# The small operations of the heads' norms on GpSimd instead of VectorE

## The chip, the cores and the metric

One core of one Trainium2 chip runs the whole program. The metric is the device time of one execution in microseconds. Lower is better.

## What is computed

Two blocks follow each other on a sequence of 1024 tokens of width 1024. The change lies in the first, an attention block with two kinds of heads: 8 heads of kind A (a window of 128 tokens each way, 2 heads of keys and values, rotary positions) and 8 heads of kind B (a neighbourhood on a grid, a bias by relative place). Both also see 256 context tokens. Ahead of the scores every head of q and k is normalised over its 64 columns:

```
q_a = _axial_rope(_rms_norm(q_a, qn_a), row_pos, col_pos)
k_a = _axial_rope(_rms_norm(k_a, kn_a), row_pos, col_pos)
q_b, k_b = _rms_norm(q_b, qn_b), _rms_norm(k_b, kn_b)
def _rms_norm(x, g):
    y = x * rsqrt(mean(x * x, axis=-1) + 1e-6)
    return y * g
```

Behind the attention come the output projection, a gated feed-forward product, and the second block.

## The kernel before, in words

Products are done in pairs of fp32r numbers, a high part and the rest, so a projection of one tile of 128 tokens is 8 slices of k with three matmuls each (`mm3`, L159 to L161).

The attention runs in six rounds (`ROUNDS`): A, B, B, B, B, A. In each, `Round.proj` projects ten tiles of 128 tokens: two of the context, eight of x. An A tile of x has 5 heads to normalise (4 of q, 1 of k), a B tile 4; a context tile has only its k, 1 or 2 heads. That makes 60 tiles, each of which calls `qk_prep` (L380). In it

- VectorE multiplies the projection by the gains (`yg`, L389 or L392), ScalarE squares it (L395), VectorE sums the squares of each head (`ssq`, L396);
- `rstd_of` (L138) makes the factor of each head: VectorE makes the mean (`ms`, L140), ScalarE takes the logarithm and the exponential (L142, L144), and VectorE does one Newton step in three operations (L146, L147, L149) on tiles of 128 by 1 to 5 columns;
- in A tiles of x GpSimd applies the rotary tables in four operations (L400, L405 twice, L407);
- VectorE multiplies by the factor (L409), ScalarE rounds the high part (L411), VectorE takes the rest (L412). Then PE transposes k and q (L491, L502).

While round r+1 is projected, the jobs of round r (one per head and tile of queries) are done: scores on PE (L548), a reduction for the maximum on VectorE (L555, L560, L563, L566), the exponential on ScalarE (L569), transposes on PE (L582), their split by ScalarE and VectorE (L592, L593), the product with v (L606), its sum (L612, L613) and a transposition back (L620). The transposes of a tile are handed in `TR_LAG` = 3 jobs after its projection. During the last round the weights of the output projection are prepared too, partly on GpSimd (L754, L172, on 128 by 1024).

`rstd_of` has two other kinds of callers, which stay as they are: the norms of whole rows (L275 and, for the first two tiles, ahead of the output projection) and the second block (L1510). Each engine does its instructions in one order. The program text gives a priority, and a scheduler with costs of its own sets the final order of each engine when the program is built, so an edit in one helper can move instructions everywhere in the stretch.

Of the kernel before, what the change touches and what calls it, by code (L numbers as in the profile page):

```python
# [12 lines left out]
ALU = mybir.AluOpType  # L13
# [8 lines left out]
HD = 64  # L22
# [5 lines left out]
EPS = 1e-6  # L28
# [52 lines left out]
def net_kernel(ctx: ExitStack, tc: tile.TileContext, I: dict, out: bass.AP):  # L81
    nc = tc.nc
    sync = nc.sync
    dve = nc.vector
    act = nc.scalar
    pool = nc.gpsimd
# [37 lines left out]
    def fview(ap):  # L124
        return ap.bitcast(F32)
# [9 lines left out]
        o, n = VECS[name]  # L135
        return vecs[:, o : o + n]

    def rstd_of(ssq, n, cols):  # L138
        ms = small.tile([P, 8], F32, tag="ms", name="ms")[:, :cols]
        dve.tensor_scalar(ms, ssq, 1.0 / n, EPS, ALU.mult, ALU.add)  # L140
        ln = small.tile([P, 8], F32, tag="ln", name="ln")[:, :cols]
        act.activation(ln, ms, AF.Ln)  # L142
        y0 = small.tile([P, 8], F32, tag="y0", name="y0")[:, :cols]
        act.activation(y0, ln, AF.Exp, scale=-0.5)  # L144
        y2 = small.tile([P, 8], F32, tag="y2", name="y2")[:, :cols]
        dve.tensor_tensor(y2, y0, y0, ALU.mult)  # L146
        dve.scalar_tensor_tensor(y2, y2, -0.5, ms, ALU.mult, ALU.mult)  # L147
        r = small.tile([P, 8], F32, tag="r", name="r")[:, :cols]
        dve.scalar_tensor_tensor(r, y2, 1.5, y0, ALU.add, ALU.mult)  # L149
        return r  # L150

    def eng(c):
        return dve if c == "d" else pool
# [32 lines left out]
    def rstd_ssq(ssq, n, cols):  # L186
        ms = small.tile([P, 8], F32, tag="ms", name="ms")[:, :cols]
        dve.tensor_scalar(ms, ssq, 1.0 / n, EPS, ALU.mult, ALU.add)
        return rstd_sqrt(ms, cols)
# [76 lines left out]
    def norm_in(src, where="xt"):  # L266
        if where == "xt":
            xt = pro.tile([P, D], F32, tag="xt", name="xt", bufs=3)
        else:
            xt = ap1.tile([P, CTX + S], F32, tag="kT", name="xk", bufs=4)[:, :D]  # L270
        sync.dma_start(xt, src)
        junk = pro.tile([P, D], F32, tag="junk", name="junk")
        ssq = small.tile([P, 8], F32, tag="ssq", name="ssq")
        act.activation(junk, xt, AF.Square, accum_out=ssq[:, 0:1])
        r = rstd_of(ssq[:, 0:1], D, 1)  # L275
        dve.tensor_scalar(xt, xt, r, None, ALU.mult)
        return xt
# [102 lines left out]
    def qk_prep(ps, g, rtile):  # L380

        n = ps.shape[1]

        def pa(name):
            return ap1.tile([P, 5, HD], F32, tag="pa", name=name, bufs=PA_BUFS)[:, :n]

        yg = pa("yg")
        if g.shape[1] == n:
            dve.tensor_tensor(yg, ps, g, ALU.mult)  # L389
        else:  # L390
            pairs = [v.rearrange("p (a b) d -> p a b d", b=2) for v in (yg, ps)]
            dve.tensor_tensor(*pairs, g.unsqueeze(2).to_broadcast([P, n // 2, 2, HD]), ALU.mult)  # L392
        sq = pa("sq")
        ssq = small.tile([P, 8], F32, tag="ssq", name="ssq")
        act.activation(sq, ps, AF.Square)  # L395
        dve.tensor_reduce(ssq[:, :n], sq, AX.X, ALU.add)  # L396
        r = rstd_of(ssq[:, :n], HD, n)
        if rtile is not None:
            t1, t2 = pa("t1"), pa("t2")
            eng(ROPE2[0]).tensor_tensor(t1, yg, tabs[0][:, 0, rtile, :].unsqueeze(1).to_broadcast([P, n, HD]), ALU.mult)  # L400
            ys = yg.rearrange("p h (e r f) -> p h e r f", e=2, r=2)
            ts_ = t2.rearrange("p h (e r f) -> p h e r f", e=2, r=2)
            sn = tabs[0][:, 1, rtile, :].rearrange("p (e r f) -> p e r f", e=2, r=2)
            for rr in range(2):
                eng(ROPE_ENG).tensor_tensor(ts_[:, :, :, rr, :], ys[:, :, :, 1 - rr, :],  # L405
                                            sn[:, :, rr, :].unsqueeze(1).to_broadcast([P, n, 2, 16]), ALU.mult)
            eng(ROPE2[2]).tensor_tensor(t1, t1, t2, ALU.add)  # L407
            yg = t1
        eng(Y_ENG).tensor_tensor(yg, yg, r.unsqueeze(2).to_broadcast([P, n, HD]), ALU.mult)  # L409
        qk = ap1.tile([P, 5, 2, HD], F32R, tag="qk", name="qk")[:, :n]  # L410
        act.copy(qk[:, :, 0, :], yg)  # L411
        eng(QLO_ENG).tensor_tensor(qk[:, :, 1, :], yg, fview(qk[:, :, 0, :]), ALU.subtract)  # L412
        return qk

    class Round:
# [44 lines left out]
        def proj(self, t, is_ctx, later):  # L460
# [3 lines left out]
            for k in range(KT):  # L464
# [9 lines left out]
                if k < KT - 1:  # L474
                    yield
            kt = t if is_ctx else 2 + t
            h0 = nq if is_ctx else 0
            n = nh - h0
            qk = qk_prep(ps[:, h0 * 64 : nh * 64].rearrange("p (h d) -> p h d", d=HD), self.g[:, h0 * self.g.shape[1] // nh :, :],
                         t if (self.kind == "A" and not is_ctx) else None)  # L480
            for j in range(nk):
# [288 lines left out]
    for s in range(-2, nj):  # L770
# [16 lines left out]
        for i, c in enumerate(ORDER):  # L787
# [18 lines left out]
            else:  # L806
                n = -(-left // ORDER[i:].count("f"))
# [358 lines left out]
    cols = {}  # L1166
# [223 lines left out]
    class Gla:  # L1390
# [64 lines left out]
        def mix(self):  # L1455
# [52 lines left out]
            ssq = small.tile([P, 8], F32, tag="ssq", name="ssq")  # L1508
            dve.tensor_reduce(ssq[:, :4], sq.rearrange("p b (h d) -> p (b h) d", h=2), AX.X, ALU.add)
            r = rstd_of(ssq[:, :4], P, 4)  # L1510
            for h in range(4):
                cs_ = slice(h * P, (h + 1) * P)
# [144 lines left out]
    cols = {}  # L1657
# [7 lines left out]
    for t in range(NT):  # L1665
# [15 lines left out]
        ssq = small.tile([P, 8], F32, tag="ssq", name="ssq")  # L1681
        act.activation(y, ps, AF.Square, accum_out=ssq[:, 0:1])
        r = rstd_ssq(ssq[:, 0:1], D, 1)
# [156 lines left out]
```

## Time and profile before

| | us |
|---|---|
| median of 3 runs | 2499.37 |
| lowest, highest | 2494.01, 2502.66 |
| the profiled execution, its own time | 2503.15 |
| its span in the profile | 2501.4 |
| PE, VectorE, ScalarE, GpSimd busy | 2395.9, 1783.5, 1217.0, 344.1 |

The span is what the trace covers, from the first instruction to the last; 1.75 us of the execution lie around it. A busy share is a mean over stages: the attention takes about the first 670 us, the first feed-forward and everything behind it the rest. In names, POOL is GpSimd, DVE VectorE, ACT ScalarE; "idle before" is the time in which the engine stood ahead of such instructions.

### The profile page before, as it was taken

The numbers are of one execution on the slowest core, as the hardware profiler recorded it, in microseconds if no ns is written. First come the engines' busy times: TensorE is split into PE (matmuls) and PEld (weight loads), VectorE is DVE, ScalarE is ACT, GpSimd is POOL, SyncE is SP. The second block draws the span as 40 slices with busy tenths as digits, with TensorE's granted clock in tenths as the row PEclk, the third lists the DMA queues.
The fourth block names the chain that finished last, engine by engine and source line by source line (L and its number), as shares of the span: only waits on it lengthen the run. The fifth ranks groups of instructions, "written<-read, shape, count | busy, mean of one in ns | idle before, by whom it ended". The sixth has DMA issues, their size and how long they took to land.

```text
span 2501.4 us, 35470 instructions
## 1 busy us (share of the span) xinstructions
PE 2395.9 (96%) x12448; PEld 2008.3 (80%) x12448; DVE 1783.5 (71%) x3636; ACT 1217.0 (49%) x2658; POOL 344.1 (14%) x340
## 2 busy tenths in 40 slices
PE   8899999999897999999999999999989999999998
PEld 4789999988775888888788888878767888788886
DVE  6977788888866877777575943437668666677676
ACT  4777677777744332233244542346335444444442
POOL 1400000023321222222000000003102221100011
PEclk9999999999999999999999999999999999999999
DMA  7111122222331343332699540022313544599973
GB/s 267 41 47 45 52 61 60 70 83 71 118 110 53 101 139 121 124 106 89 225 333 302 191 129 17 22 59 79 104 54 126 168 145 140 197 344 329 301 241 138
DMA packets 202893, 337.89 MB, mean 135 GB/s; under 512 B 22846, under 2 KB 84174, under 8 KB 201692
## 3 DMA queue, kind: packets, MB, share of 16 engines
q1 hardware_dynamic: 200700, 328.30, 39.3%
q0 software_dynamic: 2016, 7.34, 0.9%
q8 instruction: 98, 1.61, 0.3%
q14 instruction: 79, 0.65, 0.1%
HBM read 265.03 MB, written 70.53 MB: 134 GB/s over the span
## 4 chain that ended last, share of the span: by engine, by line
PE 80%; DVE 9%; ACT 5%; DMA 2%; issue 2%; SPq 0%; POOL 0%; DVEq 0%; ACTq 0%; POOLq 0%
PE m L160 14%; PE m L161 14%; PE m L159 14%; PE acc L159 4%; PE acc L161 4%; PE acc L160 4%; PE wide L159 3%; PE wide L160 3%; PE wide L161 3%; PE acc L606 2%; PE tr L582 2%; PE wide L548 2%; ACT qT L156 1%; PE tr L160 1%; PE tr L161 1%
## 5 line engine op out<-in xcount | busy, mean ns | idle before, releaser
L159 PE MATMUL m<-T,s 128*128 128x512 f32 x1064 | 416.9, 393 | 30.5 <-ACT T L890 25.0
L160 PE MATMUL m<-T,s 128*128 128x512 f32 x1064 | 417.9, 393 | 0.0
L161 PE MATMUL m<-T,s 128*128 128x512 f32 x1064 | 417.5, 393 | 0.0
L890 ACT CAST slab<-cmb 128x1024 fp32r<-128x1024 f32 x189 | 193.1, 1047 | 261.4 <-DVE cmb L1103 111.0
L891 DVE TENSOR_TENSOR slab<-cmb,slab 128x1024 fp32r<-128x1024 f32 x189 | 229.8, 1237 | 105.3 <-ACT slab L890 100.7
L890 ACT CAST s<-raw 128x512 fp32r<-128x512 f32 x228 | 136.1, 615 | 263.3 <-PE m L161 94.8
L159 PEld LDWEIGHTS m<-T,s 128*128 128x128 f32 x1064 | 201.3, 189 | 75.9 <-ACT T L890 25.8
L891 POOL TENSOR_TENSOR s<-raw,s 128x512 fp32r<-128x512 f32 x114 | 159.3, 1399 | 617.4 <-ACT s L890 604.0
L160 PE MATMUL m<-slab 128*128 128x512 f32 x594 | 234.0, 394 | 5.9 <-DVE slab L891 5.9
L160 PEld LDWEIGHTS m<-T,s 128*128 128x128 f32 x1064 | 201.4, 189 | 44.8 <-DVE T L891 1.3
L161 PEld LDWEIGHTS m<-T,s 128*128 128x128 f32 x1064 | 201.3, 189 | 42.6
L161 PE MATMUL m<-slab 128*128 128x512 f32 x594 | 233.5, 393 | 0.0
L159 PE MATMUL m<-slab 128*128 128x512 f32 x594 | 231.0, 391 | 1.3 <-ACT slab L890 1.3
L990 DVE TENSOR_TENSOR big<-m,big 128x512 f32<-128x512 f32 x228 | 154.0, 682 | 57.8 <-PE m L161 53.2
L159 PE MATMUL acc<-wi,slab 128*128 128x384 f32 (+1 forms) x480 | 168.6, 352 | 3.0 <-DVE y L147 1.3
L160 PE MATMUL acc<-wi,slab 128*128 128x384 f32 (+1 forms) x480 | 161.5, 337 | 0.5 <-DVE wi L240 0.5
L161 PE MATMUL acc<-wi,slab 128*128 128x384 f32 (+1 forms) x480 | 160.9, 337 | 0.0
L593 DVE TENSOR_TENSOR PT<-tr,PT 128x512 fp32r<-128x512 f32 x231 | 129.3, 564 | 44.0 <-ACT PT L592 41.8
L592 ACT CAST PT<-tr 128x512 fp32r<-128x512 f32 x231 | 112.2, 489 | 65.5 <-PE acc L606 33.3
L160 PEld LDWEIGHTS m<-slab 128*128 128x128 f32 x594 | 112.9, 190 | 30.9 <-DVE slab L891 7.5
L159 PEld LDWEIGHTS m<-slab 128*128 128x128 f32 x594 | 111.9, 188 | 25.1 <-ACT slab L890 1.7
L161 PEld LDWEIGHTS m<-slab 128*128 128x128 f32 x594 | 112.8, 190 | 23.3
(455 smaller groups left out, 5288.0 us busy)
## 6 DMA issues: line engine op xcount, KB each, us to landing
cmb<-scr SPq DMA_DIRECT2D x189, 256.0 KB, 4.2
wraw<-in_w_ff_dram SPq DMA_DIRECT2D x160, 256.0 KB, 5.4
scr<-big SPq DMA_DIRECT2D x135, 256.0 KB, 4.0
wraw<-in_w_down_dram SPq DMA_DIRECT2D x110, 256.0 KB, 5.1
raw<-in_w_ff_dram SPq DMA_DIRECT2D x16, 1024.0 KB, 6.5
scr<-big SPq DMA_DIRECT2D x27, 512.0 KB, 6.7
wm<-in_w_mod_dram SPq DMA_DIRECT2D x48, 256.0 KB, 2.7
raw<-in_w_gate_dram SPq DMA_DIRECT2D x11, 1024.0 KB, 5.4
```

What stands on the lines that cost most here:

```text
L156: act.copy(out_, in_) if c == "a" else eng(c).tensor_copy(out_, in_)
L159: pe.matmul(ps, lhsT=l_hi, rhs=r_hi, start=first, stop=False)
L160: pe.matmul(ps, lhsT=l_hi, rhs=r_lo, start=False, stop=False)
L161: pe.matmul(ps, lhsT=l_lo, rhs=r_hi, start=False, stop=last)
L548: pe.matmul(Sps[:, o : o + ln], lhsT=qT[:, w_, :], rhs=R.kT[self.kh][:, src : src + ln], start=(w_ == 0), stop=(w_ == 1))
L582: pe.transpose(t[:, (j - b0) * P : (j - b0 + 1) * P], self.P_t[:, j * P : (j + 1) * P], ident)
L592: act.copy(PT[:, :, 0, :], src)
L593: dve.tensor_tensor(PT[:, :, 1, :], src, fview(PT[:, :, 0, :]), ALU.subtract)
L606: pe.matmul(OT, lhsT=R.V[self.kh][:, vt, :], rhs=self.PT[j // 4][:, j % 4].rearrange("p e t -> p (e t)"), start=(j == 0), stop=(j == nk_al ...
L890: act.copy(hi, src)
L891: eng(lo_eng).tensor_tensor(lo, src, fview(hi), ALU.subtract)
L990: dve.tensor_tensor(V[:, half], ps, getattr(self, other[0])[:, other[1]], ALU.add)
```

## The change

The call in `qk_prep` hands GpSimd to `rstd_of`. GpSimd then does the mean and the Newton step. The two fused operations of VectorE become three plain ones, so five operations on GpSimd stand for four on VectorE. The other callers keep VectorE.

```
@@ -135,18 +135,24 @@
         o, n = VECS[name]
         return vecs[:, o : o + n]
 
-    def rstd_of(ssq, n, cols):
+    def rstd_of(ssq, n, cols, e=None):
+        e = e or dve
         ms = small.tile([P, 8], F32, tag="ms", name="ms")[:, :cols]
-        dve.tensor_scalar(ms, ssq, 1.0 / n, EPS, ALU.mult, ALU.add)
+        e.tensor_scalar(ms, ssq, 1.0 / n, EPS, ALU.mult, ALU.add)
         ln = small.tile([P, 8], F32, tag="ln", name="ln")[:, :cols]
         act.activation(ln, ms, AF.Ln)
         y0 = small.tile([P, 8], F32, tag="y0", name="y0")[:, :cols]
         act.activation(y0, ln, AF.Exp, scale=-0.5)
         y2 = small.tile([P, 8], F32, tag="y2", name="y2")[:, :cols]
-        dve.tensor_tensor(y2, y0, y0, ALU.mult)
-        dve.scalar_tensor_tensor(y2, y2, -0.5, ms, ALU.mult, ALU.mult)
         r = small.tile([P, 8], F32, tag="r", name="r")[:, :cols]
-        dve.scalar_tensor_tensor(r, y2, 1.5, y0, ALU.add, ALU.mult)
+        e.tensor_tensor(y2, y0, y0, ALU.mult)
+        if e is dve:
+            dve.scalar_tensor_tensor(y2, y2, -0.5, ms, ALU.mult, ALU.mult)
+            dve.scalar_tensor_tensor(r, y2, 1.5, y0, ALU.add, ALU.mult)
+        else:
+            e.tensor_tensor(y2, y2, ms, ALU.mult)
+            e.tensor_scalar(y2, y2, -0.5, 1.5, ALU.mult, ALU.add)
+            e.tensor_tensor(r, y2, y0, ALU.mult)
         return r
 
     def eng(c):
@@ -394,7 +400,7 @@
         ssq = small.tile([P, 8], F32, tag="ssq", name="ssq")
         act.activation(sq, ps, AF.Square)
         dve.tensor_reduce(ssq[:, :n], sq, AX.X, ALU.add)
-        r = rstd_of(ssq[:, :n], HD, n)
+        r = rstd_of(ssq[:, :n], HD, n, pool)
         if rtile is not None:
             t1, t2 = pa("t1"), pa("t2")
             eng(ROPE2[0]).tensor_tensor(t1, yg, tabs[0][:, 0, rtile, :].unsqueeze(1).to_broadcast([P, n, HD]), ALU.mult)
```

On the engines that makes 240 instructions fewer on VectorE and 300 more on GpSimd; the counts of PE, ScalarE and of the DMAs stay. The order on all engines changes up to about the first feed-forward product and is the same from there on.

VectorE at a B tile (the fifth tile of x of the fourth round, from just behind its `ssq`; L409 is the product with the factor, L566 the reduction of a job's scores). Before:

```order
L485 TENSOR_TENSOR V<-acc,V 128x64
L140 TENSOR_SCALAR ms<-ssq 128x4
L613 TENSOR_TENSOR ob<-ob,acc 128x128
L563 TENSOR_REDUCE mx<-wide 128x1
L146 TENSOR_TENSOR y_5393<-y_5391 128x4
L485 TENSOR_TENSOR V<-acc,V 128x64
L147 SCALAR_TENSOR_TENSOR y_5393<-y_5393,ms 128x4
L566 ISA wide,negs<-wide,tbl,mx 128x512
L566 ISA negs 128x1
L149 SCALAR_TENSOR_TENSOR r<-y_5393,y_5391 128x4
L593 TENSOR_TENSOR PT<-tr,PT 128x4x128
L409 TENSOR_TENSOR yg<-yg,r 128x256
```

Of the change, whose lines here stand 6 further down, from its `ssq` (L402) on; L415 is the product with the factor, L572 the reduction:

```order
L402 TENSOR_REDUCE ssq<-sq 128x4
L491 TENSOR_TENSOR V<-acc,V 128x64
L619 TENSOR_TENSOR ob<-ob,acc 128x128
L569 TENSOR_REDUCE mx<-wide 128x1
L491 TENSOR_TENSOR V<-acc,V 128x64
L415 TENSOR_TENSOR yg<-yg,r 128x256
L572 ISA wide,negs<-wide,tbl,mx 128x512
L572 ISA negs 128x1
L599 TENSOR_TENSOR PT<-tr,PT 128x4x128
```

The product with the factor now stands ahead of the reduction of the scores and of the split of the transposes, with four instructions between it and `ssq` where eleven stood.

GpSimd at the third tile of x of the last round. Before:

```order
L754 TENSOR_TENSOR tbl<-tbl,g1t 128x1024
L400 TENSOR_TENSOR t_8069<-yg,rope 128x320
L405 TENSOR_TENSOR t_8070<-yg,rope 128x10x16 x2
L407 TENSOR_TENSOR t_8069<-t_8069,t_8070 128x320
L754 TENSOR_TENSOR tbl<-tbl,g1t 128x1024
L172 TENSOR_TENSOR slab<-tbl,slab 128x1024 x2
```

Of the change, where L760 is what L754 was and L178 what L172 was:

```order
L406 TENSOR_TENSOR t_8124<-yg,rope 128x320
L411 TENSOR_TENSOR t_8125<-yg,rope 128x10x16 x2
L413 TENSOR_TENSOR t_8124<-t_8124,t_8125 128x320
L141 TENSOR_SCALAR ms<-ssq 128x5
L760 TENSOR_TENSOR tbl<-tbl,g1t 128x1024 x2
L148 TENSOR_TENSOR y_8118<-y_8116 128x5
L153 TENSOR_TENSOR y_8118<-y_8118,ms 128x5
L154 TENSOR_SCALAR y_8118<-y_8118 128x5
L155 TENSOR_TENSOR r<-y_8118,y_8116 128x5
L178 TENSOR_TENSOR slab<-tbl,slab 128x1024 x2
```

The rotary operations now come ahead of both weight products, the mean follows them, and the rest of the factor comes behind both.

## Rows read from the trace of the kernel before

**Rows 1.** The page: busy time of each engine, share of the span, instructions.

```profile
PE 2395.9 (96%) x12448; PEld 2008.3 (80%) x12448; DVE 1783.5 (71%) x3636; ACT 1217.0 (49%) x2658; POOL 344.1 (14%) x340
```

**Rows 2.** Windows: stretch, length, busy us of PE, PEld, DVE, ACT, POOL, clock, DMA.

```profile
40.00:100.00 60.00, 49.70 (x271) 42.74 (x271) 55.46 (x175) 42.28 (x128) 30.03 (x39) 0.89 0.30 106
150.00:500.00 350.00, 344.08 (x2411) 323.94 (x2410) 276.16 (x900) 244.92 (x786) 7.80 (x33) 1.00 0.19 52
500.00:660.00 160.00, 144.31 (x985) 129.36 (x985) 141.03 (x375) 124.94 (x352) 53.16 (x59) 0.97 0.23 72
```

**Rows 3.** Waits of PE, 100 to 680 us: total us, times, longest.

```profile
PE tr L582 <- DVE PT L593: 4.7, 7, 1.7
...
PE tr L491 <- DVE qk L412: 3.0, 1, 3.0
```

**Rows 4.** Groups by form, 0 to 1100 us: busy us, mean ns, idle before.

```profile
L140 DVE TENSOR_SCALAR ms<-ssq 128x4 f32<-128x4 f32 x32 | 5.2, 163 | 0.0
L146 DVE TENSOR_TENSOR y<-y 128x4 f32<-128x4 f32 x32 | 5.2, 161 | 3.8 <-ACT y L144 3.6
...
L149 DVE SCALAR_TENSOR_TENSOR r<-y,y 128x4 f32<-128x4 f32 x32 | 5.0, 156 | 0.1
L147 DVE SCALAR_TENSOR_TENSOR y<-y,ms 128x4 f32<-128x4 f32 x32 | 4.9, 153 | 0.0
```

**Rows 5.** Groups by form, VectorE, 500 to 660 us (the last A round).

```profile
L149 DVE SCALAR_TENSOR_TENSOR r<-y,y 128x5 f32<-128x5 f32 x8 | 5.5, 682 | 0.0
...
L140 DVE TENSOR_SCALAR ms<-ssq 128x5 f32<-128x5 f32 x8 | 4.3, 535 | 0.0
...
L147 DVE SCALAR_TENSOR_TENSOR y<-y,ms 128x5 f32<-128x5 f32 x8 | 2.2, 275 | 0.0
...
L146 DVE TENSOR_TENSOR y<-y 128x5 f32<-128x5 f32 x8 | 2.0, 253 | 0.2
```

**Rows 6.** Timeline around one B tile: start, us, engine, line, instruction.

```profile
382.36 0.41 DVE L396 TENSOR_REDUCE ssq<-sq 128x4 f32<-128x256 f32 x1
...
383.72 0.16 DVE L146 TENSOR_TENSOR y<-y 128x4 f32<-128x4 f32 x1 [0.22 <-ACT y L144]
...
384.01 0.75 DVE L566 CUSTOM_DVE_ANT_0 wide<-wide,tbl,mx 128x512 f32<-128x512 f32 x1
...
384.97 0.91 ACT L569 ACTIVATE prob<-wide,negs 128x768 f32<-128x768 f32 x1
...
385.71 0.42 DVE L409 TENSOR_TENSOR yg<-yg,r 128x256 f32<-128x256 f32 x1
...
389.38 0.82 PE L582 MATMUL tr<-ident,prob 128*128 128x128 f32 x6
```

**Rows 7.** Timeline of POOL, 500 to 700 us.

```profile
555.04 2.37 POOL L754 TENSOR_TENSOR tbl<-tbl,g1t 128x1024 f32<-128x1024 f32 x1 [13.90 <-ACT tbl L753]
557.36 0.88 POOL L400 TENSOR_TENSOR t<-yg,rope 128x320 f32<-128x320 f32 x1
...
562.49 2.35 POOL L172 TENSOR_TENSOR slab<-tbl,slab 128x1024 fp32r<-128x1024 f32 x1
566.87 2.40 POOL L172 TENSOR_TENSOR slab<-tbl,slab 128x1024 fp32r<-128x1024 f32 x1 [2.03 <-ACT slab L169]
...
641.12 0.29 POOL L589 CAST PT<-pf 128x128 fp32r<-128x128 f32 x1
641.49 0.46 POOL L590 TENSOR_TENSOR PT<-pf,PT 128x128 fp32r<-128x128 f32 x1
```

**Rows 8.** The chain that ended last, pieces in the last A round: start, us, what.

```profile
560.39 2.16 DVE r L149
562.65 2.54 DVE t L409
...
623.95 2.07 DVE r L149
...
635.88 1.50 DVE ms L140
```

More of the change, by code (lines that the diff above doesn't have):

```diff
@@ L136, in vec, with rstd_of @@
         return vecs[:, o : o + n]
-    def rstd_of(ssq, n, cols):
+    def rstd_of(ssq, n, cols, e=None):
+        e = e or dve
         ms = small.tile([P, 8], F32, tag="ms", name="ms")[:, :cols]
-        dve.tensor_scalar(ms, ssq, 1.0 / n, EPS, ALU.mult, ALU.add)
+        e.tensor_scalar(ms, ssq, 1.0 / n, EPS, ALU.mult, ALU.add)
         ln = small.tile([P, 8], F32, tag="ln", name="ln")[:, :cols]
@@ L145, in rstd_of @@
         y2 = small.tile([P, 8], F32, tag="y2", name="y2")[:, :cols]
-        dve.tensor_tensor(y2, y0, y0, ALU.mult)
-        dve.scalar_tensor_tensor(y2, y2, -0.5, ms, ALU.mult, ALU.mult)
         r = small.tile([P, 8], F32, tag="r", name="r")[:, :cols]
-        dve.scalar_tensor_tensor(r, y2, 1.5, y0, ALU.add, ALU.mult)
+        e.tensor_tensor(y2, y0, y0, ALU.mult)
+        if e is dve:
+            dve.scalar_tensor_tensor(y2, y2, -0.5, ms, ALU.mult, ALU.mult)
+            dve.scalar_tensor_tensor(r, y2, 1.5, y0, ALU.add, ALU.mult)
+        else:
+            e.tensor_tensor(y2, y2, ms, ALU.mult)
+            e.tensor_scalar(y2, y2, -0.5, 1.5, ALU.mult, ALU.add)
+            e.tensor_tensor(r, y2, y0, ALU.mult)
         return r
@@ L396, in qk_prep @@
         dve.tensor_reduce(ssq[:, :n], sq, AX.X, ALU.add)
-        r = rstd_of(ssq[:, :n], HD, n)
+        r = rstd_of(ssq[:, :n], HD, n, pool)
         if rtile is not None:
```

## The prediction

> **What bounds the kernel now.** I read the page's busy times first: PE is busy for 2395.9 of 2501.4 us, VectorE for 71% and GpSimd for 14% [rows 1]. So PE bounds the whole, and moving work from VectorE pays only where VectorE keeps PE waiting. The windows show where that can be. From 150 to 500 us, the B rounds, PE is busy for 344.1 of 350 us and VectorE for 276.2: there is 5.9 us to win at most. From 40 to 100 us VectorE is busy for 55.5 of 60 us and PE stands for 10.3; from 500 to 660 us, the last A round, VectorE is busy for 141.0 of 160 and PE stands for 15.7 [rows 2]. These two ends are where the change can act. From the first feed-forward on nothing is moved.
>
> PE's list of waits then tells what a late head costs. Of all 60 tiles only one had PE wait for the end of a norm chain (transposes of k behind L412), for 3.0 us; the split of the transposes of the probabilities (L593) cost 4.7 us in 7 waits [rows 3]. So in nearly all tiles the chain of the norm has room, and a change of its length is mostly hidden.
>
> **The change, part by part.** The sum is made against the profiled execution, 2503.15 us, whose span is 2501.4; that execution is 3.8 us (0.15%) above the median of 2499.37, so I add the same difference to both.
>
> What VectorE gives up. At a 4-head tile the four operations take 163 + 161 + 156 + 153 = 633 ns [rows 4]. At the eight 5-head tiles of the last round they take 5.5 + 4.3 + 2.2 + 2.0 = 14.0 us, 1.75 us a tile, because some of them are held up [rows 5]. In the first round the eight 5-head tiles give between 8 x 0.63 = 5.0 and 14.0 us. The time VectorE stands for the exponential ahead of L146 goes too; at the B tile shown it is 0.22 us [rows 6].
>
> What GpSimd takes on. No GpSimd operation on so few columns is in the trace. Two inputs of 128 columns take 0.46 us and of 320 columns 0.88, so 2.2 ns a column; going from 128 columns down to 4 leaves 0.19 us. One input of 128 columns takes 0.29. The dependent one behind it starts 0.08 us after its end [rows 7]. I take 0.19 us for each of the five and 0.08 for each handover; the row at 128 columns bounds it above at 0.46, and below it cannot be under zero. GpSimd gets 60 x 5 x 0.19 = 57 us of work, with room for it.
>
> A page speaks against this: the Trainium skill, GPSIMD Engine Reference, section 4.1 (Engine selection), says elementwise operations of two inputs are about twice as slow there and belong on VectorE. At 128 columns and more the rows lean that way; at 4 columns the estimate by rows is 0.19 against VectorE's 0.16. By the page each operation would take 0.32 us, an estimate that makes each chain about 0.5 us longer and the forecast some 4 us higher.
>
> The B tiles, 40 of them. At the tile shown `ssq` ends at 382.77, and L146 starts at 383.72, as ScalarE ends the factor's exponential at about 383.7 [rows 6]. Before, L409 starts at 385.71. Now the mean goes out through GpSimd (0.08 + 0.19 + 0.08 = 0.35), which still meets ScalarE's place in its order; then four operations (4 x 0.19 + 3 x 0.08 = 1.0) and two handovers of 0.08 put the factor at 384.85. L409 can start 0.9 us earlier than before. But VectorE reaches L409 earlier still: its new order leaves four instructions behind `ssq`. The old order had these four, three of the small operations and 0.22 us of idle time before L566 started at 384.01; less the idle time and between nothing and 3 x 0.16, that is 383.3 to 383.8, and I take 383.6. VectorE stands there for 1.25 us, and saved 0.63 + 0.22 = 0.85 at most: it loses 0.4 us a tile, 16 us in 350 of which it is busy for 276, so it stays under 85%. What is queued behind L409 is late: the reduction of a job's scores (L566), which began at 384.01, now waits for L409 to end (384.85 + 0.42 = 385.27), 1.26 us later, and the exponential on ScalarE with it. PE takes the transposes of that exponential at 389.38, and it ended at 385.88 [rows 6]: 3.5 us of room against 1.3. I take **+1.5 us** for the tiles with less room, between -3 (half of the 5.9 us) and +8 (0.2 us a tile).
>
> The first 150 us. VectorE is freed of 5.0 us or more. Against it stands a wait at L409 in each of 8 A tiles, where the rotary operations and the splits of x are ahead of the factor in GpSimd's queue. As in the B tiles the wait is a little the larger, and PE, which stands for other things too, sees a part: **+1 us**, between -5 (half of PE's 10.3) and +5 (0.6 us a tile).
>
> The last A round. Here the chain that ended last runs through the moved operations themselves: L149 for 2.16 and 2.07 us, L140 for 1.50, each several times its 0.16, beside GpSimd work on 1024 columns; L409 for 2.54 beside L172 [rows 7, 8]. If all three go from the chain, that is -5.7. But one does not: behind the factor at 623.95 GpSimd's next work is again L172, which then holds L409 instead of L149; so -3.7. What comes: at the tile of 554 us two products of 2.37 us (L754) now stand between mean and Newton step. L400 started as L754 ended, so the rotary part can move up by 2.37 at most, from an end near 560.2 to 557.8; then 2 x 2.37 and 1.0 us put the factor at 563.6, where L149 ended at 562.55. That is +1.1. L409 then falls beside the first L172, as before, and L412 can fall beside the second (566.87 to 569.27), which it was ahead of: up to +2.4. Together +3.5, at the one tile where PE already waited 3.0 [rows 3, 7]. The other seven chains are longer by 0.6 us each (five operations for four, three handovers), half of it on PE's path: +2. Sum of this part **+1.8**, between -6 and +9.
>
> Scheduler's moves of other instructions, PE's included, have no term; they widen the range by 2 us each way. Sum: 1.5 + 1 + 1.8 = 4.3 us. 2503.15 + 4.3 = 2507.5 for the profiled execution, and 2499.4 + 4.3 = **2503.7** for the median.
>
> **The rivals.** *VectorE was the bound at both ends, and its relief reaches PE.* It loses 5.0 + 14.0 = 19 us where PE stands for 26. For it: the busy shares of 92 and 88% there. Against it: VectorE is made to stand at L409 instead. If half reaches PE, -9.5: 2490. Chance 0.15.
>
> *VectorE stands at L409 too long (slower).* Place: the reductions and splits behind it, hence exponentials and PE's transposes. It decides from the point where the room behind the exponential is under 1.3 us or a small GpSimd operation takes over 0.3 us instead of 0.19 (five of them add 0.55 us to each chain). The two A rounds, with PE standing already, are where room is thin. If their 16 tiles of x cost PE 0.75 us each and the tile at 554 the full 3.5, that is 15.5: 2515. Chance 0.28.
>
> *The move does nothing.* The instructions do move (240 go, 300 come), and what could make the move idle is the forecast's own case: the chain has room, and VectorE's gain is spent at L409. Chance 0.57, with a range of its own of 2495 to 2507.
>
> **How the numbers follow.** About 0.3%, 7.5 us, is what a measurement of this kernel can tell from no change. The time lies within 0.3% (2491.9 to 2506.9) in the forecast's case: 0.57. The two rivals hold the rest, 0.15 and 0.28. The range runs from 2491, just short of the faster rival's price, to 2515, the slower one's.
>
> **What would show it.** In the new profile: GpSimd operations on 4 columns near 0.19 us; some 8% less VectorE work from 150 to 500 us (40 x 0.6 of 276) but an idle time of about 1.2 us a tile ahead of L415, released by GpSimd; PE still busy for over 97% there. At the third tile of x of the last round, two L760 between mean and Newton step, and PE's wait for the transposes of k above 3 us. It would be wrong if small GpSimd operations took 0.3 us or more, if PE's busy time fell under 95% from 150 to 500 us, or if the first 100 us became shorter by over 5 us.

## The result, and the profile after

The changed kernel takes 2542.03 us (median of 4, 2539.1 to 2543.94) against 2497.6 before (median of 4, one run more than in the table above): 1.0173 times, 95% interval 1.016 to 1.0185. By this ratio it is some 43 us slower (the medians differ by 44), where I forecast 4 and ended the range at 2515. The profiled execution shown below has a span of 2540.1 us.

The page's busy line after, to be set beside [rows 1]:

```profile
PE 2408.4 (95%) x12448; PEld 2006.6 (79%) x12448; DVE 1758.6 (69%) x3396; ACT 1216.2 (48%) x2658; POOL 409.4 (16%) x640
```

VectorE gave up 24.9 us of busy time and GpSimd took on 65.3. To see where the time went I cut both traces at the same points of the program: the start of the first transposes of k of tile 10 (counted from 0: the first B tile) and of tile 50 (the first tile of the last A round), and the end of the last tile's. The windows between them, first of the kernel before, then of the change (columns: from:to, length, busy time and count of PE, PEld, DVE, ACT, POOL; granted clock, DMA share, GB/s):

```profile
0.00:168.60 168.60, 145.19 (x833) 112.42 (x834) 137.69 (x410) 109.81 (x322) 42.83 (x65) 0.95 0.38 131
168.60:517.70 349.10, 343.17 (x2411) 323.07 (x2410) 276.16 (x897) 242.47 (x773) 7.93 (x32) 1.00 0.19 54
517.70:644.70 127.00, 114.06 (x762) 103.10 (x760) 112.07 (x291) 96.17 (x263) 47.69 (x48) 0.96 0.27 83
```

```profile
0.00:175.90 175.90, 147.38 (x821) 112.88 (x821) 133.63 (x359) 109.55 (x318) 57.93 (x125) 0.93 0.36 125
175.90:550.10 374.20, 353.30 (x2422) 324.81 (x2423) 267.61 (x745) 243.00 (x775) 46.47 (x227) 1.00 0.18 51
550.10:686.20 136.10, 117.23 (x761) 103.39 (x760) 99.16 (x255) 95.77 (x263) 56.91 (x92) 0.95 0.25 77
```

The first ten tiles lose 7.3 us, the B rounds 25.1, the last A round 9.1; behind it nothing is lost (2540.1 - 686.2 = 1853.9 us against 2501.4 - 644.7 = 1856.7). The B rounds, where I saw room, lost most. The granted clock there is full in both, so it has no part. In the first ten tiles its mean was 0.95 before and 0.93 after, in the last A round 0.96 and 0.95. If TensorE alone set the pace, that would be some 3.6 and 1.3 us (an estimate from these rows: 168.6 x 0.95 / 0.93 and 127.0 x 0.96 / 0.95, less the stretch). Whether the clock fell because TensorE stood more, or for another reason, no run here shows.

A trap in reading: PE's busy time in the B rounds rose by 10.1 us for nearly the same matmuls (2411 and 2422 records), and only 15.0 of the 25.1 us show as idle time. The ends of matmuls are modelled, so a short wait disappears inside a "busy" one. The weight loads, which TensorE does ahead of its matmuls (PEld: 323.07 and 324.81 us), hardly grew, and their waits show the rest: summed over the whole list, 21.5 us before and 46.5 after in the B rounds, 25.0 us more where 25.1 are lost. The Trainium skill, Perfetto Trace Analysis (the note at its head), warns that matmul busy time is a bad measure because matmuls are pipelined; these rows agree.

The waits of the weight loads in the B rounds (what waited, for which operation: us in total, times, longest; not the whole list, but lines of it that grew), before:

```profile
PEld tr L582 <- ACT qT L156: 7.5, 20, 0.7
PEld acc L159 <- DVE V L485: 0.6, 3, 0.2
PEld acc L606 <- DVE ot L633: 0.5, 1, 0.5
PEld tr L582 <- DVE PT L593: 0.8, 2, 0.5
```

and after:

```profile
PEld tr L588 <- ACT qT L162: 12.0, 26, 0.9
PEld acc L165 <- DVE V L491: 7.5, 17, 0.9
PEld acc L612 <- DVE ot L639: 5.8, 9, 0.9
PEld tr L588 <- DVE PT L599: 4.4, 10, 0.9
PEld acc L612 <- DVE V L491: 2.1, 5, 0.7
```

No line has TensorE wait for the heads' own values (L418). Most of what grew is a wait for other VectorE work: the split of V (L491), which frees the bank of the projection, the output (L639), which frees the next accumulator, and the splits of the probabilities (L599), which free the bank of their transposes. The longest line is ScalarE's: its copies of the transposed q (L162), which free such a bank too, 7.5 us before and 12.0 after. How VectorE comes to be late is seen at one B tile; all engines, in order of start:

```profile
412.96 0.41 DVE L402 TENSOR_REDUCE ssq<-sq 128x4 f32<-128x256 f32 x1
413.69 0.19 POOL L141 TENSOR_SCALAR ms<-ssq 128x4 f32<-128x4 f32 x1
413.92 0.20 ACT L143 ACTIVATE ln<-ms 128x4 f32<-128x4 f32 x1 [0.81 <-POOL ms L141]
414.03 0.20 ACT L490 CAST V<-acc 128x64 fp32r<-128x64 f32 x1
...
414.26 0.23 DVE L491 TENSOR_TENSOR V<-acc,V 128x64 fp32r<-128x64 f32 x1
...
414.44 0.20 POOL L148 TENSOR_TENSOR y<-y 128x4 f32<-128x4 f32 x1 [0.56 <-ACT y L145]
...
414.63 0.41 PE L165 MATMUL acc<-wi,slab 128*128 128x384 f32 x1 [1.20 <-DVE V L491]
...
415.28 0.20 POOL L155 TENSOR_TENSOR r<-y,y 128x4 f32<-128x4 f32 x1
...
415.51 0.42 DVE L415 TENSOR_TENSOR yg<-yg,r 128x256 f32<-128x256 f32 x1 [1.03 <-POOL r L155]
...
415.85 0.68 DVE L599 TENSOR_TENSOR PT<-tr,PT 128x512 fp32r<-128x512 f32 x1
```

VectorE has nothing to do for 1.03 us: L415 heads its queue and GpSimd's factor is not there. The split L599 behind it could have run. ScalarE stood 0.81 us for the mean in the same way, with the second copy of V (L490) queued behind. TensorE's own wait at this tile, 1.20 us, is for the split of that copy (L491 at 414.26), which stands ahead of L415: this tile does not show what the standing costs, the experiments do. The groups of GpSimd's operations in the B rounds, by shape (busy, mean ns), and VectorE's waits at L415 and L418 there:

```profile
L148 POOL TENSOR_TENSOR y<-y 128x4 f32<-128x4 f32 x32 | 6.7, 210 | 20.1 <-ACT y L145 20.1
L141 POOL TENSOR_SCALAR ms<-ssq 128x4 f32<-128x4 f32 x32 | 6.2, 194 | 181.9 <-DVE ssq L402 163.0 <-DVE V L491 18.6
```

```profile
DVE yg L415 <- POOL r L155: 29.3, 40, 1.0
DVE qk L418 <- ACT qk L417: 0.2, 1, 0.2
```

So 29.3 us of standing in 40 tiles, 0.73 us a tile. The last A round shows the queue of GpSimd that I worked out; its operations at the third tile of x:

```profile
593.07 0.20 POOL L141 TENSOR_SCALAR ms<-ssq 128x5 f32<-128x5 f32 x1
593.35 4.70 POOL L760 TENSOR_TENSOR tbl<-tbl,g1t 128x1024 f32<-128x1024 f32 x2
598.00 0.21 POOL L148 TENSOR_TENSOR y<-y 128x5 f32<-128x5 f32 x1
```

Both products L760 stand between mean and Newton step, and VectorE stood 3.05 us at L415 for it:

```profile
599.08 0.49 DVE L415 TENSOR_TENSOR t<-t,r 128x320 f32<-128x320 f32 x1 [3.05 <-POOL r L155]
```

TensorE's waits in the last A round say what was late there: not the transposes of k, as I had thought (their 3.0 us of [rows 3] are gone), but the splits of the probabilities, 3.0 us in 2 waits before. Now:

```profile
PE tr L588 <- DVE PT L599: 9.4, 8, 2.9
```

### The profile page after: what moved, and what is told of

Same layout as the page of the kernel before. It is cut to its first block, busy times and chain, and to the rows that moved or that the text cites. A ratio compares the mean times of both kernels' runs of the same rounds, so it can differ in the third digit from the quotient of the medians.

```text
span 2540.1 us, 35483 instructions
## 1 busy us (share of the span) xinstructions
PE 2408.4 (95%) x12448; PEld 2006.6 (79%) x12448; DVE 1758.6 (69%) x3396; ACT 1216.2 (48%) x2658; POOL 409.4 (16%) x640
## 4 chain that ended last, share of the span: by engine, by line
PE 75%; DVE 9%; ACT 6%; POOL 4%; issue 2%; DMA 2%; SPq 0%; DVEq 0%; ACTq 0%; POOLq 0%
PE m L166 14%; PE m L167 14%; PE m L165 14%; PE acc L165 4%; PE acc L167 4%; PE acc L166 4%; PE wide L165 3%; PE wide L167 3%; PE wide L166 3%; PE acc L612 2%; PE tr L588 2%; ACT qT L162 1%; PE tr L166 1%; PE tr L165 1%; PE tr L167 1%
## 5 line engine op out<-in xcount | busy, mean ns | idle before, releaser
L599 DVE TENSOR_TENSOR PT<-tr,PT 128x512 fp32r<-128x512 f32 x231 | 129.2, 563 | 47.9 <-ACT PT L598 46.5
L588 PE MATMUL tr<-ident,prob 128*128 128x128 f32 x720 | 119.9, 282 | 26.8 <-DVE PT L599 14.4
L897 DVE TENSOR_TENSOR s<-raw,s 128x512 fp32r<-128x512 f32 x114 | 93.6, 821 | 63.4 <-ACT s L896 63.3
L166 PEld LDWEIGHTS m<-slab 128*128 128x128 f32 x594 | 111.9, 188 | 29.6 <-DVE slab L897 6.7
```

Source lines behind the costliest of these rows:

```text
L166: pe.matmul(ps, lhsT=l_hi, rhs=r_lo, start=False, stop=False)
L588: pe.transpose(t[:, (j - b0) * P : (j - b0 + 1) * P], self.P_t[:, j * P : (j + 1) * P], ident)
L599: dve.tensor_tensor(PT[:, :, 1, :], src, fview(PT[:, :, 0, :]), ALU.subtract)
L897: eng(lo_eng).tensor_tensor(lo, src, fview(hi), ALU.subtract)
```

## The experiments

Two theories. **Standing**: VectorE stands at L415 for GpSimd, and what is queued behind is late. **Order**: the scheduler, given another program, put all engines' instructions into another order, and that costs whether or not anything stands. Each run is told beside the 2497 to 2500 us of the kernel before that ran with it.

**e1_no_wait.**

```
-        eng(Y_ENG).tensor_tensor(yg, yg, r.unsqueeze(2)...)
+        eng(Y_ENG).tensor_tensor(yg, yg, ssq[:, :n].unsqueeze(2)...)
```

> The normalising product (L415) takes ssq, VectorE's own sum, in place of the factor r; GpSimd still works out r for every tile, but nobody reads it (left out: the true scaling of q and k). Theory 'standing' (VectorE stands at L415 for GpSimd's r, 29.3 us in 40 tiles of the B rounds, and the splits, reductions and outputs queued behind it are late for TensorE): the loss goes, 2485 to 2505 us. Rival 'order' (what costs is the new order of the other instructions, or GpSimd's work as such, standing or not): 2530 us or more.

Measured: 2525.26, 1.0106 (1.0091 to 1.0121), between the two ranges: 17 us came back, 26 did not. But this program was scheduled anew too, so it settles nothing alone.

**e2_yg_pool.**

```
-Y_ENG = "d"
+Y_ENG = "p"
```

> The normalising product L415 goes to GpSimd too, so VectorE has nothing to stand for between ssq and the split L418. GpSimd takes some 0.7 us on 256 columns where VectorE took 0.42, so each chain is longer by 0.3 us. Theory 'standing': 2505 to 2525, since VectorE can do the splits of V and the score reductions in that time and meets only L418. Rival 'late heads' (TensorE waits for the transposes of q and k because the chain is longer): 2550 or more. Rival 'order': 2530 to 2550.

Measured: 2551.39, 1.0213 (1.0198 to 1.0229). My theory's number was wrong, and so was its premise: VectorE was not set free. It stood at L418 instead, for ScalarE's copy of GpSimd's product (its waits in the B rounds, which lost 24.9 us):

```profile
DVE qk L418 <- ACT qk L417: 42.3, 38, 2.2
```

This program was scheduled anew too, so it does not tell standing from order.

**e3_a_only.**

```
-        r = rstd_of(ssq[:, :n], HD, n, pool)
+        r = rstd_of(ssq[:, :n], HD, n, pool if g.shape[1] == n else dve)
```

> Only the 20 tiles of the two A rounds have the small operations on GpSimd; the 40 of the B rounds have them on VectorE as before. Comparing the starts of each tile's transposes of k in both traces, the first 175 us lose 7 us, the B rounds 25, the last A round 9. If the losses are local ('standing'): 2542 - 25 = 2517, between 2510 and 2523. If the loss is one of a whole new order, it can fall anywhere: 2500 or 2540.

Measured: 2519.06, 1.0077 (1.0061 to 1.0094). As expected of local losses, they stay where GpSimd has the small operations: B rounds -0.2 us, the first tiles +7.6, the last A round +8.2.

**e4_longer.**

```
             e.tensor_scalar(y2, y2, -0.5, 1.5, ALU.mult, ALU.add)
+            e.tensor_scalar(y2, y2, 1.0, 0.0, ALU.mult, ALU.add)
+            e.tensor_scalar(y2, y2, 1.0, 0.0, ALU.mult, ALU.add)
             e.tensor_tensor(r, y2, y0, ALU.mult)
```

> GpSimd's part gets two more dependent operations (a product with 1.0 twice), 2 x 0.28 = 0.56 us more for every tile; VectorE's work stays. Theory 'standing': VectorE stands 0.56 us longer in each of 60 tiles, 34 us, of which TensorE sees 0.6 to 0.85 as it did of the first 0.75 us: 2562 to 2571. Rival 'order': 2535 to 2550.

Measured: 2560.38, 1.0242 (1.0225 to 1.0259): 18 us more than the change, under the 20 to 29 expected. Its order differs little from the changed kernel's (in the traces, by line, tile and shape, at 241 of 12448 places on TensorE), so most of this is the price of 34 us more in the chains: about half is seen.

**Orders held.** To part the two theories I held the order: at the end of the program, edges that only set the order of issue chain the instructions of each engine as a table says; the small operations are left out of the table and are placed freely. In the traces TensorE's matmuls stand, told by line, tile and shape, at every place as before in p1 and as in the change in p2 and p3. No run holds a kernel to its own order and changes nothing else; but f2 below, held so, was faster than the kernel before, so the holding itself shows no price.

```
+def hold_order(tc, nc):
...
+    for e, t in ORDERS.items():
...
+        for a, b in zip(seq, seq[1:]):
+            tc.add_manual_dep(b, a.name, nosync, reason="order")
```

**p1_pool_old_order.**

> The changed kernel (small operations on GpSimd), with every other instruction held, on each engine, in the order that it had before: only the 300 GpSimd operations are placed freely. Theory 'order' (most of the loss comes from the order that the scheduler made of the changed program): the loss goes, 2490 to 2510 us, since before VectorE came to L409 later than GpSimd's factor would be there (worked out: 385.71 against 384.85 at the tile of 382 us). Theory 'GpSimd itself' (handovers, heads late whatever the order): 2525 us or more. Theory 'half and half' (the kernel without the wait got back 17 of the 43 us): 2510 to 2525.

**p2_dve_new_order.**

> The kernel before (small operations on VectorE), with every other instruction held in the order of the changed kernel on each engine. Theory 'order': 2520 to 2545 us although nothing is on GpSimd. Theory 'standing for GpSimd only': 2495 to 2505. With VectorE's own four operations between ssq and L409 the wait there is for ScalarE's logarithm and exponential alone, so part of the standing can remain.

**p3_new_order_no_wait**, with e1's edit.

> The changed kernel, all instructions held in its own order, but L415 takes ssq in place of r (r is worked out and not read; the scaling of q and k is left out). Against the changed kernel (2542 us) this takes away the standing at L415 and nothing else. Theory 'standing': 2495 to 2510. Theory 'order': 2530 to 2542. The earlier kernel without the wait, in an order of its own, took 2525.

**c_unfused_dve.**

> Control: all five small operations on VectorE, unfused as on GpSimd (60 more VectorE operations of 0.16 us, 10 us of VectorE's work), scheduled freely. Theory 'any new order costs': 2515 us or more, though nothing is handed over to GpSimd. Theory 'the handover or VectorE's place at L409 costs': 2498 to 2510, some 0.1 us a tile.

Measured, with the ratio to the kernel before:

| small operations | old order | new order |
|---|---|---|
| VectorE | 2499.34 (before) | 2516.33 (p2), 1.0064 (1.0049 to 1.0079) |
| GpSimd | 2508.28 (p1), 1.0039 (1.0027 to 1.0051) | 2542.03 (the change) |
| GpSimd, L415 does not wait for the factor | | 2514.6 (p3), 1.0053 (1.0038 to 1.0068) |

GpSimd alone costs 9 us, the new order alone 17, and both together 43: 17 us arise only where they meet. p1 fell in the range of theory 'order', p2 and p3 between the ranges of the two: neither theory holds alone. In the new order the wait is worth 2542 - 2514.6 = 27 us. The control c_unfused_dve, with nothing on GpSimd and ten us more VectorE work, took 2518.66, 1.007 (1.0053 to 1.0087): a rescheduled program lost 19 us without any handover, in the range of 'any new order costs'; TensorE's order differs from that of before at 1393 places. The added work may be a part of it; no run has that work in the old order.

By the same cuts as above, against the kernel before (us; "standing" is VectorE's at L415 for GpSimd and at L418 for ScalarE's copy, in the B rounds, or at the same two operations where the lines differ; a dash: not there or under what the view lists):

| run | first ten tiles | B rounds | last A round | standing |
|---|---|---|---|---|
| the kernel before | 0 | 0 | 0 | - + 6.0 |
| the change | +7.3 | +25.1 | +9.1 | 29.3 + 0.2 |
| p1 | +1.8 | -2.3 | +7.6 | 6.7 + 5.3 |
| p2 | +2.4 | +15.9 | -1.4 | - + 1.1 |
| p3 | -1.3 | +8.1 | +2.9 | - + 5.1 |

The waits of the weight loads in the B rounds, summed as above, follow these losses: 21.5 us before, 46.5 in the change, 20.2 in p1, 36.2 in p2, 29.0 in p3. Between the change and p3 only the wait differs, so their lists show which of TensorE's waits L415 causes in the B rounds. In p3:

```profile
PEld tr L588 <- ACT qT L162: 10.2, 23, 0.9
PEld acc L165 <- DVE V L491: 6.4, 12, 0.9
PEld tr L588 <- DVE PT L599: 2.0, 8, 0.3
```

The waits of L612 for the output (5.8 us) are gone, those for the splits of the probabilities are 2.0 us in place of 4.4 at L588, and those for ScalarE's copies of q fall by 1.8. The wait of the projection for the split of V stays (6.4 of 7.5): in the change it is the order's, not L415's.

In the old order the B rounds lose nothing (2.3 us less, small in a single trace): in most tiles L415 comes up when the factor is there (waits of VectorE in p1, B rounds):

```profile
DVE yg L415 <- POOL r L155: 6.7, 12, 0.8
DVE qk L418 <- ACT qk L417: 5.3, 10, 1.3
```

Most of p1's loss is in the last A round, where GpSimd's queue is full. Its rows at the tile that was at 554 us before:

```profile
564.72 2.38 POOL L760 TENSOR_TENSOR tbl<-tbl,g1t 128x1024 f32<-128x1024 f32 x1 [1.36 <-ACT tbl L759]
567.06 0.19 POOL L148 TENSOR_TENSOR y<-y 128x5 f32<-128x5 f32 x1
...
568.05 2.42 POOL L178 TENSOR_TENSOR slab<-tbl,slab 128x1024 fp32r<-128x1024 f32 x1
```

```profile
568.13 2.68 DVE L415 TENSOR_TENSOR t<-t,r 128x320 f32<-128x320 f32 x1 [2.49 <-POOL r L155]
```

The Newton step waited for L760, VectorE stood 2.49 us for it, and L415 then took 2.68 us beside L178 on GpSimd, as L409 did in [rows 8].

**f1_one_place.** p1 with another table; the order on VectorE at one of the 40 tiles, against p1's:

```
 L491 TENSOR_TENSOR V<-acc,V 128x64
+L415 TENSOR_TENSOR yg<-yg,r 128x128
 L561 ISA wide,negs<-wide,tbl,nsink 128x640
 L561 ISA negs 128x1
 L639 TENSOR_TENSOR ot<-acc,rec 128x256
 L633 TENSOR_TENSOR es<-negs,sink 128x4
-L415 TENSOR_TENSOR yg<-yg,r 128x128
```

> As p1 (GpSimd, all orders as before), but for one instruction of each of the 40 B tiles: L415 stands on VectorE where L146 stood, one to four places earlier (three in most). There ScalarE's exponential has come and GpSimd's four operations (4 x 0.20 + 3 x 0.08 = 1.04 us) have still to run. Theory 'place of the waiting instruction': VectorE stands about 0.7 us more in 40 tiles, of which TensorE sees half, +10 to +20 on p1: 2518 to 2528. Theory 'the rest of the order': 2506 to 2512.

Measured: 2550.83, 1.0202 (1.0186 to 1.0217): 42 us more than p1, by one instruction moved one to four places. The standing is 46.4 us, 1.2 a tile, and the B rounds are 41.0 us longer than p1's for 39.7 us more of it: all of the addition reaches TensorE. In most of the tiles (not in the one shown) the second split of V is what now stands right behind L415. VectorE's waits and TensorE's in the B rounds:

```profile
DVE yg L415 <- POOL r L155: 46.4, 38, 1.6
```

```profile
PE acc L165 <- DVE V L491: 21.7, 17, 2.3
PE acc L612 <- DVE V L491: 10.0, 11, 1.3
```

My number for it (0.7 us more a tile, half of it seen) was too low on both counts: it is 1.0 more, and all is seen.

**f2_b_only_old_order.** p1 and

```
-        r = rstd_of(ssq[:, :n], HD, n, pool)
+        r = rstd_of(ssq[:, :n], HD, n, pool if g.shape[1] != n else dve)
```

> Small operations on GpSimd in the 40 tiles of the B rounds only, VectorE in the two A rounds, all orders as before. By the starts of the tiles, p1 gained 2.3 us in the B rounds and lost 1.8 and 7.6 us in the two A rounds. Theory 'local': 2499.4 - 2.3 = 2497, between 2493 and 2500, so at best a little faster than both kernels.

Measured: 2494.41, 0.9981 (0.9971 to 0.9991). This beats both kernels, by 5 us (0.2%) against the one before: little, but the interval lies clear of 1.

**f4_longer_old_order.** e4's diff, and the old order held.

> p1 with two more dependent GpSimd operations in every tile (+0.56 us each chain), all orders as before. In the new order the same addition cost 18 us. Theory 'the room behind the factor decides': VectorE stood 6.7 us in 12 of the 40 B tiles in p1, so the added 0.56 us is met in part: +4 to +12 us, 2512 to 2520. Theory 'a longer chain costs as such': +18, 2526.

Measured: 2518.21, 1.0074 (1.006 to 1.0088): +9.9 on p1, where the same addition cost 18 in the new order; standing at the normalising product rose from 6.7 to 15.7 us.

**g1_pe_order_only.** The kernel before; of the table only this is kept:

```
+ORDERS = {"PE": ...}
```

> The kernel before (small operations on VectorE) with TensorE's order alone held as in the changed kernel; the other engines' orders are made to fit it. With all engines held so it took 2516. Theory 'it is TensorE's order': 2510 to 2520. Theory 'it is the order on VectorE and ScalarE': 2498 to 2506.

Measured: 2524.16, 1.0099 (1.0085 to 1.0113). This is above the range that I had given TensorE's order, and more than with all engines held so (p2). TensorE's order is enough to lose; that it is the only part doesn't follow, as the other engines were ordered anew around it.

**Moves in the new order.** The change with its own order held, but for the second copy of V on ScalarE (h1), L415 (h3), both (h4), or L415 and L418 (h5). ScalarE in h1 and VectorE in h3, at one tile each, against the change:

```
+L490 CAST V<-acc 128x64
 L143 ACTIVATE ln<-ms 128x2
-L490 CAST V<-acc 128x64
```

```
+L491 TENSOR_TENSOR V<-acc,V 128x64
+L619 TENSOR_TENSOR ob<-ob,acc 128x128
+L561 ISA wide,negs<-wide,tbl,nsink 128x640
+L561 ISA negs 128x1
 L415 TENSOR_TENSOR yg<-yg,r 128x128
-L491 TENSOR_TENSOR V<-acc,V 128x64
-L619 TENSOR_TENSOR ob<-ob,acc 128x128
-L561 ISA wide,negs<-wide,tbl,nsink 128x640
-L561 ISA negs 128x1
```

The second fence also shows what the change had queued behind L415 at that tile: a split of V, a sum and a score reduction.

**h1_v_copy_first.**

> The changed kernel, all orders its own, but for ScalarE in the 40 B tiles: the second copy of V (L490) stands ahead of the logarithm L143, one to three places earlier than it did. In the B rounds ScalarE stood 6.6 us at L143 for GpSimd's mean and TensorE waited 6.6 us for the splits of V that follow this copy. Theory 'V behind the logarithm': that wait goes, 2530 to 2537. Theory 'V late for another reason': 2540 to 2545.

**h3_l415_later.**

> The changed kernel, all orders its own, but for VectorE in the 40 B tiles: L415 stands one to three places later (two in most, never behind its L418). Theory 'place of the waiting instruction': of the 29.3 us of standing some 20 go and TensorE gets back about half, 2528 to 2535. Theory 'the rest of the order': 2538 to 2545.

**h4_both.**

> Both moves at once, all else in the changed kernel's order. If the two stand for different parts of the B rounds' 25 us, the gains add: 2516 to 2530. The loss of the last A round (9 us) and the first 176 us (7 us) stay, so it can't come under 2515 by these moves.

**h5_both_later.**

> As h3 (new order, L415 one to three places later on VectorE in the 40 B tiles), and L418 three places later too. In h3 the standing moved: 3.2 us at L415 but 17.6 at L418, which waits for ScalarE's copy of L415's product. Theory 'the standing is what costs, at either instruction' (new order without any wait lost 8.1 us in the B rounds; the changed kernel, 29.5 us of standing, 25.1): with some 9 us of standing left, 8.1 + 0.58 x 9 = 13 us lost in the B rounds, 2524 to 2532. Theory 'the loss is in the order whatever stands': 2535 to 2540.

Measured: h1 2547.78, 1.0199 (1.0184 to 1.0215); h3 2538.16, 1.0169 (1.0152 to 1.0186); h4 2538.19, 1.0166 (1.0151 to 1.0182); h5 2534.36, 1.0149 (1.0132 to 1.0166). The kernel before ran 2496.8 beside them. h1 and h4 came out above every range given, h3 in that of 'the rest of the order', h5 between its two. h1 put the copy first and so the logarithm, the factor and L415 later: standing at L415 rose to 36.4 us and the B rounds lost 30.6, while TensorE waited for the split of V as long as in the change (5.7 us against 5.6). In h3 the standing moved on by one instruction (VectorE's waits, B rounds):

```profile
DVE qk L418 <- ACT qk L417: 17.6, 37, 1.0
DVE yg L415 <- POOL r L155: 3.2, 9, 0.7
```

and the B rounds lost 19.6. With L418 moved too (h5) its wait is gone from the list, 3.2 us at L415 remain, and the B rounds lose 15.9, which is what p2 lost with nothing on GpSimd, and more than the 13 expected. So about 9 of the 25 us are the places of these two instructions. What the new order costs beyond them is settled only so far: in h5 ScalarE stands 22.8 us at L417 for L415 (8.0 before, 11.2 in the change), ahead of its other work, and TensorE still waits 6.9 us for the split of V. Why the new order holds that split up is open.

## Why the prediction was wrong, step by step

- **GpSimd's price was right.** Estimated 0.19 us for each operation and 0.08 between; measured 0.194 to 0.210 and, at the tile shown, 0.08 to 0.09. From the start of L148 to the end of L155 it takes 1.04 us; I had 1.0.
- **VectorE's standing in the B rounds was over-estimated,** 1.25 us a tile against 0.73. So was its relief: I summed the four records to 0.63 us a tile and expected 8% less work, but its busy time fell by 8.6 us (276.16 to 267.61), 3%. The records of neighbours overlap, as these of the kernel before do, so their sum is more than the operations hold of the engine:

```profile
382.82 0.16 DVE L140 TENSOR_SCALAR ms<-ssq 128x4 f32<-128x4 f32 x1
382.89 0.28 DVE L613 TENSOR_TENSOR ob<-ob,acc 128x128 f32<-128x128 f32 x1
```

- **The page:** the rule of the Trainium skill that I weighed (GPSIMD Engine Reference, section 4.1, Engine selection: twice as slow) does not hold at 4 columns, where these rows show 0.20 against VectorE's 0.153 to 0.163 [rows 4]; it was not what cost. I had also put it on all five operations, and two of them have one input.
- **The step that failed: "What is queued behind L409 is late: the reduction of a job's scores (L566) ... 3.5 us of room against 1.3".** I followed one queued instruction, which had room, to its end, and priced the B rounds at +1.5. The standing itself cost 17.0 us there: they lose 25.1 in the change and 8.1 in p3, where only the wait is gone. What TensorE felt were others: by the lists of these two, the output, which frees the accumulator that TensorE writes next, and the splits of the probabilities; and where the split of V stands behind L415, that one (f1: 31.7 us of such waits). In f1 all of the added standing was seen, so they have no such room. The bound of +8 was 0.2 us a tile, a guess at what TensorE would see; of the standing it saw 0.4, of the whole change 0.6. My own sign of being wrong came true: PE was busy for 94.4% of the B rounds (353.30 of 374.20 us), under the 95% that I had named.
- **The second step that failed: "Scheduler's moves of other instructions ... have no term".** The order alone cost 17 us (p2), and a control with one more VectorE operation a tile, and the new order that came of it, cost 19. Meeting the wait, it cost another 17.
- **The last A round:** mechanism right, size not. I worked out L760 between mean and Newton step and L415 beside L178, and took +1.8 of a bound of +9. Measured: +9.1, and +7.6 in the old order. At the third tile of x VectorE stood 3.05 us, and what was late for TensorE were the splits of the probabilities (9.4 us), not the transposes of k. The gain of 3.7 us that I set against it shows in neither total.
- **The first 150 us:** +1 forecast, bound +5; measured +7.3, of which the old order keeps 1.8; without the wait the new order loses nothing there (p3: -1.3).
- **The rival "VectorE stands at L409 too long"** was the right mechanism for a part: the wait is worth 27 us (p3), where I had 15.5, most of it in the B rounds and not in the A rounds, and it came although GpSimd's small operations took 0.2 us, under the 0.3 that I had made one of its two conditions. The order's 17 us were in no rival.

## What to carry to other kernels

Before an operation that was cheap is sent to another engine, look at the queue of the engine that takes the result back: the price is the time that this engine stands at the head of its queue, times the share of it that the bottleneck feels through what is queued behind (here TensorE, through splits and outputs that free a PSUM bank). Where a scheduler orders the program, a change of engine is two changes; hold the old order to see the operation's own price, which here was 9 us of 43, and a gain in the rounds where GpSimd was free (f2).

## What was not expected of the hardware

- A GpSimd operation on 128x4 takes 0.194 to 0.210 us, only 0.03 to 0.05 more than VectorE's, and the next dependent one starts 0.08 us behind its end.
- TensorE can lose 25 us in a stretch while its busy time grows by 10: its ends are modelled, and a part of the waiting is counted as work. The waits of the weight loads show it: they sum to 25.0 us more.
- L415, 0.49 us on 128x320 when GpSimd is quiet (599.08 us in the change), took 2.68 us in p1 where GpSimd began a subtraction on 128x1024 (L178) 0.08 us ahead of it. The Trainium skill, SBUF — State Buffer (Who interferes with whom), says that a VectorE instruction with two SBUF inputs contends with a GpSimd instruction that reads SBUF; the row agrees.
